# Splits off GpSimd, a second q on ScalarE, and attention steps at other places among the projection's units

## The chip, the cores and the metric

The kernel runs on one core of one Trainium2 chip. The metric is the device time of one execution in microseconds (us), the median of several. Engines are TensorE (PE, with its weight loads as PEld), VectorE (DVE), ScalarE (ACT), GpSimd (POOL) and SyncE (SP), whose queue issues nearly all transfers.

## The reference

A decoder block on 256 tokens of 1024 numbers, float32: an attention mixer, a layer norm, a mixture of 32 experts, a second layer norm. Cut to what matters here:

```python
proj = x @ w_in + b_in                       # q, k, v of mixers A and B, gates
y_a = banded_attention(qa, ka, va, bias_a, 128, sinks)
y_b = g0 * o_cmp + g1 * o_slc + g2 * o_win   # compressed, selected, window branches of mixer B
merged = gate_a * (y_a @ w_branch_a) + gate_b * (y_b @ w_branch_b)
h = layer_norm(alpha * x + merged @ w_out)
logits = h @ w_router + b_router             # top 4 of 32 experts
for each expert e and its tokens:
    u = rows @ w_gate_up[e] + b_gate_up[e]
    out += weight * (swiglu(u) @ w_down[e] + b_down[e])
y = layer_norm(alpha * h + out)
```

Expert weights are 12.6 MB for each of 32 experts, and all are read once.

## The kernel before

The front computes the projection in 32 **units**, n = 0 to 31: a unit is 128 of the 4096 columns, in the order of `order` (four of qa, k, v, two for the compressed branch, k, four of qb, v, k, v, and 16 merge gates). From unit 2 on the product is made of three matmuls for each of 8 row blocks, with x and w each split in a high part (rounded to fp32r) and a low part (the rest), so 24 matmuls of 128x256 in a unit. `split_w` makes these parts for unit n + 2 while unit n runs (`AHEAD`): `round_split` (L193) casts the high part on ScalarE and subtracts on DVE; where `POOL_PART` says "h" GpSimd makes the high part (L196), where it says "l" GpSimd subtracts (L200). Three pairs of weight tiles take turns (`NWS`).

A unit yields after its fourth and after its eighth row block. These **steps** h = 0 to 63 are where the attention's work is put in: `PLAN` names for each step what is called there. `Sbr` is the scores of branch b (0 is mixer A, 1 the selected branch, 2 the window) and head pair r: eight matmuls into two of three PSUM banks (`ps_s`), four DVE operations that add the bias and take the maximum, four exponentials on ScalarE. `N` is the norm (reciprocal on DVE, four multiplications on GpSimd), `T` six transposes on TensorE and two copies, `V` the product with V into the one bank of `ps_y`, which is read as `y` before the next `V`. `vt` are V's transposes, `cp` the compressed branch's products, `ct` a transpose (`pct`), `bl`, `bs`, `bw`, `br` the load, split, store and reload of the experts' biases, `sig` the sigmoids of the first four merge gates, `bias1` the load of a Toeplitz bias.

In this loop only TensorE's and SP's instructions stand in the order in which the code calls them; those of DVE, ScalarE and GpSimd are placed by a scheduler, for the most part as their inputs are expected to be there. Every engine runs its own instructions in order.

At step `END_H` the attention's buffers are given back, and three slots of 2 MB for expert weights (`ringb`) stand in their place. `PRE` says at which steps loads of expert weights are issued ahead; ten slots can be filled before the experts run. After the units come the branch products (`pb`), the output projection (`po`), the router, and the experts in turn, each with four loads of 2 MB (`wg`) and two (`wd`). All of these loads stand in SP's queue in one order, each waiting for its slot.

Of the kernel before, what the change touches and what calls it, by code (L numbers as in the profile page):

```python
# [20 lines left out]
P = 128  # L21
# [12 lines left out]
NRA, NRB, NRP = 3, 3, 1  # L34
WARM = 6
NWS, NSB, AHEAD, SIG0 = 3, 6, 2, 20
POOL_PART = {6: 'h', 7: 'l', 8: 'h', 9: 'l', 10: 'h', 11: 'h', 12: 'h', 14: 'h', 15: 'h', 16: 'l', 17: 'l', 18: 'l', 19: 'h', 20: 'h', 21: 'h', 22: 'h', 23: 'h', 24: 'h', 25: 'h', 27: 'l', 28: 'l', 30: 'l', 38: 'l'}
SIDE_R = "right"
LOADS, LOADS2 = 6, 11
END_H = 36  # L40
SPLIT = 672
SPLIT1 = 512
AHEAD2 = (2, 2, 2, 2, 2, 2, 1, 0)
# [1 line left out]
TWO = 4  # L45
LN_ROWS = {9 + i: (0, i) for i in range(4)} | {20 + i: (1, i) for i in range(4)}
E_RES = 13
PLAN = {7: 'gates', 8: 'sinks', 9: 'c1', 10: 'gsum S00 S02', 11: 'S01 N00 N01', 12: 'N02', 13: 'T00 S03 N03 bias1 T02', 14: 'vt0 V00 T01', 15: 'V01 blocks', 16: 'V02 T03', 17: 'V03 mlp bl', 19: 'gelu', 20: 'bs', 22: 'bw', 23: 'ckv S10 N10', 24: 'S11 N11 br', 26: 'S12 T10 N12', 27: 'T11 S13 N13', 28: 'vt1 csm', 29: 'T12 V11 S20', 30: 'V10 T13 N20', 31: 'ct V13 vt2', 32: 'S21 V12 T20 cp1 cp0 S22 N22 V20 S23', 33: 'N21 T21 N23', 34: 'cp2 cp3 V21 T22', 35: 'rw V22 T23', 36: 'x V23', 38: 'sel', 39: 'sig'}
PRE = {26: 1, 39: 1, 41: 1, 48: 1, 64: 1, 71: 1, 72: 2, 73: 2}


C_BQA, C_BQB, C_BK, C_BV, C_BC, C_PK, C_W2K, C_W2V, C_WN = 0, 4, 8, 11, 14, 16, 48, 112, 176
# [7 lines left out]
def tile_block(ctx: ExitStack, tc: tile.TileContext, a, out):  # L60
    nc = tc.nc
    PE, DVE, ACT, POOL, SP = nc.tensor, nc.vector, nc.scalar, nc.gpsimd, nc.sync
# [124 lines left out]
    mp = er.enter_context(tc.tile_pool(name="mp", bufs=1, side=SIDE_R))  # L187
# [67 lines left out]
    pk = mp.tile([P, NPK], F32, name="pk")  # L255
# [67 lines left out]
    qT = {}  # L323
# [37 lines left out]
    def prep(n):  # L361
        while prepped[0] <= min(n, len(jobs) - 1):
            k = prepped[0]
            prepped[0] += 1
            parts[k] = split_w(jobs[k](), f"j{k}", POOL_PART.get(k, ""), 2 if k < TWO else 1)

    z2 = []
    mg = {}
    def unit(n):

        issue(n + (LOADS if n < 10 else 12))
        if n >= MAN:
            prep(n + AHEAD)

        wh, wl = parts.pop(n) if n >= MAN else (chunk(0)[:, n], None)
        k = order[n]
        t = w_tile(f"pu{n}")
        for j in range(NJ):
            if n < MAN:
                PE.matmul(t[:, :S], wh[:, j, :], xT[:, j, :], start=(j == 0), stop=(j == NJ - 1))  # L380
            else:
                mm3(t[:, :S], wh[:, j, :], wl[:, j, :], xh[:, j, :], xl[:, j, :], j == 0, j == NJ - 1)
            if j == 3:
                yield
        t = t[:, :S]
        if k[0] == "q":
            c = (C_BQA, C_BQB)[k[1]] + k[2]
            if k[2] == 0:
                qT[k[1]] = mp.tile([P, 4, S], F32, tag="qT", name=f"qT{k[1]}")
            DVE.tensor_scalar(qT[k[1]][:, k[2], :], t, pk[:, c:c + 1], 0.125, ALU.add, ALU.mult)  # L390
        elif k[0] == "k":
            b = k[1]
            kT[b] = mp.tile([P, S + 15], F32, tag=f"kT{b % 2}", name=f"kT{b}")
            ACT.activation(kT[b][:, kof[b]:kof[b] + S], t, AF.Identity, bias=pk[:, C_BK + b:C_BK + b + 1])
        elif k[0] == "v":
            b = k[1]
            vt = pp.tile([P, S], F32, tag="vt", bufs=1, name=f"vt{b}")
            ACT.activation(vt, t, AF.Identity, bias=pk[:, C_BV + b:C_BV + b + 1])
            vts[b] = vt
        elif k[0] == "c":  # L400
            if not z2:
                z2.append(mp.tile([P, 2, 2, P], F32, tag="tz", name="z2"))

            s = k[1]
            tv = t.rearrange("p (u two) -> p two u", two=2)
            for par in range(2):
                for g in range(2):
                    DVE.tensor_scalar_add(z2[0][64 * par:64 * par + 64, s, g, :], tv[64 * g:64 * g + 64, par, :],
                                          pk[64 * g:64 * g + 64, C_BC + s:C_BC + s + 1])
# [19 lines left out]


    bd = dram.tile([3, P, 768], BF16, name="bd")
    bt = []

    def bias_load():
        bt.append(mp.tile([P, 2048], F32, name="bt"))
        SP.dma_start(bt[0][:, :512], a["b_gu"].rearrange("e (q c) -> (e q) c", q=4))
        SP.dma_start(bt[0][:, 512:768], a["b_d"].rearrange("e (q c) -> (e q) c", q=4))

    def bias_split():
        f = bt[0][:, :768]  # L440
        b3 = bt[0][:, 768:1920].bitcast(BF16).rearrange("p (k c) -> p k c", k=3)
        for k in range(3):
            (DVE.tensor_copy if k == 2 else ACT.copy)(b3[:, k], f)
            if k < 2:
                DVE.tensor_tensor(f, f, b3[:, k], ALU.subtract)

    def bias_store():
        b3 = bt[0][:, 768:1920].bitcast(BF16).rearrange("p (k c) -> p k c", k=3)
        SP.dma_start(bd.rearrange("k p c -> p k c"), b3)

    def bias_rows():
        SP.dma_start(bparts, bd.rearrange("k (e q) c -> (k e) (q c)", q=4))
# [273 lines left out]
    for b in range(3):  # L726
        steps[f"vt{b}"] = lambda b=b: v_transpose(b)
        steps[f"bias{b}"] = lambda b=b: load_T(b)
        for r in range(4):
            p = pairs[b][r]  # L730
            steps[f"S{b}{r}"], steps[f"N{b}{r}"], steps[f"T{b}{r}"], steps[f"V{b}{r}"] = p.scores, p.norm, p.transpose, p.pv
    for r in range(4):
        steps[f"cp{r}"] = lambda r=r: cmp_pv(r)
    plan = {k: [steps[x] for x in v.split()] for k, v in PLAN.items()}
    h = 0
    for n in range(len(order)):
        for _ in unit(n):
# [12 lines left out]
    for mt in range(8):  # L750
        if mt % 2 == 0:
            n = len(order) + mt
            issue(n + 1 + LOADS2)
            prep(n + 1 + AHEAD)
            wb = [parts.pop(n), parts.pop(n + 1)]
        preload(PRE.get(64 + mt, 0))
        t = w_tile(f"pb{mt}")
        k = (mt % 2) * P
# [7 lines left out]
        if mt % 4 == 3:  # L766
# [16 lines left out]
    sel = cp.tile([P, 2, E], F32, name="sel")  # L783
# [360 lines left out]
    for e in range(E):  # L1144
        x, p = ex[e], (ex[e - 1] if e else None)
# [88 lines left out]
    with tc.For_i(0, nrun, 1) as e:  # L1234
# [13 lines left out]
        for tt in range(2):  # L1248
            t_ = slice(tt * P, (tt + 1) * P)
            for jj in range(2):  # L1250
                t = ps_w.tile([P, 512], F32, tag="w0", name=f"vht{tt}{jj}")
# [5 lines left out]
            for hf in range(2):  # L1257
# [7 lines left out]
                t = ps_w.tile([P, 512], F32, tag="w0", name=f"vt{tt}{hf}")  # L1265
# [116 lines left out]
```

## Time and profile before

| | us |
|---|---|
| median of 3 runs | 1139.63 (1136.96 to 1140.21) |
| the profiled execution | 1138.73 |
| its span | 1137.0 |
| start of unit 18's second half, behind the last attention step | 118.32 |
| end of the units | 157.3 |

Times in the profile count from the start of the span. The busy share of TensorE counts an engine's instructions from start to end, and matmuls overlap, so it is an upper bound of work.

### The profile page before, as it was taken

What the parts mean: (1) busy time and instruction counts of PE and PEld (TensorE: products, weight loads), DVE (VectorE), ACT (ScalarE), POOL (GpSimd) and SP (SyncE); (2) the same over time, 40 slices, a digit from 0 to 9 for tenths busy, and PEclk for the clock granted to TensorE, in tenths of its full rate; (3) what the DMA queues carried; (4) which work ended last, traced back from release to release, by engine and by line L of the source; (5) the groups of instructions that cost most, each with busy time, mean ns of one, the idle gap of its engine ahead of it and who ended that gap; (6) DMA issues with size and microseconds to landing.
All of it is one profiled execution on the core that took longest, in us unless ns stands there. A gap on an engine that the chain in (4) does not pass through costs nothing.

```text
span 1137.0 us, 13456 instructions
## 1 busy us (share of the span) xinstructions
PE 1069.5 (94%) x5660; PEld 511.0 (45%) x5660; DVE 293.1 (26%) x710; ACT 203.8 (18%) x434; POOL 78.9 (7%) x115
## 2 busy tenths in 40 slices
PE   9799999999999999999999998998999998989895
PEld 7686998643434343434343333333333333333321
DVE  3777447312111111111121211111020202010213
ACT  3446244220111011111110101010111110001011
POOL 1435310000000000000000000000000000000001
PEclk9899999999999999899999999999999999999998
DMA  8562777699999999999999999999999999999993
GB/s 317 208 243 115 316 295 305 264 423 427 428 426 428 427 428 427 428 426 429 426 427 427 429 427 427 427 428 427 428 426 428 427 428 426 428 427 428 428 427 126
DMA packets 36848, 438.50 MB, mean 386 GB/s; under 512 B 3872, under 2 KB 6576, under 8 KB 9008
## 3 DMA queue, kind: packets, MB, share of 16 engines
q1 hardware_dynamic: 36448, 436.98, 92.0%
q8 instruction: 46, 0.75, 0.3%
q10 hardware_dynamic: 336, 0.62, 0.2%
q14 instruction: 18, 0.15, 0.0%
HBM read 435.92 MB, written 1.66 MB: 385 GB/s over the span
## 4 chain that ended last, share of the span: by engine, by line


## 5 line engine op out<-in xcount | busy, mean ns | idle before, releaser
L1099 PE MATMUL g<-wg,xeM 128*64 128x512 f32 x2048 | 474.7, 604 | 3.7 <-DMA wg<-in_w_gu_dram 3.6
L1099 PEld LDWEIGHTS g<-wg,xeM 128*64 128x64 f32 x2048 | 141.3, 138 | 265.2 <-issue 236.6
L1121 PE MATMUL pd<-wd,wk 128*64 128x512 f32 x1024 | 228.9, 594 | 28.7 <-DMA wd<-in_w_d_dram 28.7
L1121 PEld LDWEIGHTS pd<-wd,wk 128*64 128x64 f32 x1024 | 73.7, 137 | 174.3 <-issue 140.2
L1126 DVE COPY y<-pd 64x512 f32<-64x512 f32 x32 | 22.2, 693 | 428.6 <-ACT y L1125 428.6
L1079 DVE TENSOR_SCALAR gs<-g 128x512 f32<-128x512 f32 x32 | 22.1, 692 | 246.7 <-PE g L1099 246.7
L1125 ACT COPY y<-pd 64x512 f32<-64x512 f32 x32 | 18.5, 578 | 296.1 <-PE pd L1121 296.1
L224 PE MATMUL pu<-xhl,w_j 128*128 128x256 f32 x240 | 70.7, 294 | 0.0
L225 PE MATMUL pu<-xhl,w_j 128*128 128x256 f32 x240 | 68.4, 285 | 0.0
L226 PE MATMUL pu<-xhl,w_j 128*128 128x256 f32 x240 | 68.3, 285 | 0.0
L1013 POOL TENSOR_SCALAR wk<-const,posm 128x64 f32<-128x64 f32 x30 | 12.8, 445 | 798.0 <-PE pst L1068 793.9
L1054 PEld LDWEIGHTS px<-wk,h_tok 128*128 128x128 f32 x480 | 55.8, 191 | 24.3 <-DVE gs L1079 12.2
L1054 PE MATMUL px<-wk,h_tok 128*128 128x128 f32 x480 | 61.6, 281 | 0.0
L1075 PE MATMUL yac<-y,wk 128*128 128x512 f32 x128 | 59.2, 605 | 0.7 <-ACT y L1125 0.7
L1110 ACT COPY wk<-pa 128x512 f32<-128x512 f32 x32 | 18.8, 586 | 196.8 <-PE pa L1109 185.3
L224 PEld LDWEIGHTS pu<-xhl,w_j 128*128 128x128 f32 x240 | 46.6, 194 | 2.0 <-issue 1.2
L225 PEld LDWEIGHTS pu<-xhl,w_j 128*128 128x128 f32 x240 | 46.5, 194 | 0.0
L226 PEld LDWEIGHTS pu<-xhl,w_j 128*128 128x128 f32 x240 | 46.4, 194 | 0.0
L1081 ACT ACTIVATE wk<-gs 128x512 f32<-128x512 f32 x31 | 19.5, 629 | 149.3 <-DVE gs L1079 149.2
L1075 PEld LDWEIGHTS yac<-y,wk 128*128 128x128 f32 x128 | 23.0, 189 | 36.7 <-issue 34.7
L1000 ACT ACTIVATE xeM<-px,const 128x128 f32<-128x128 f32 x64 | 24.1, 457 | 74.5 <-PE px L1054 73.1
L202 DVE TENSOR_TENSOR w_j<-w,w_j 128x1024 fp32r<-128x1024 f32 (+1 forms) x24 | 29.1, 1222 | 25.9 <-ACT w_j L198 15.3
(230 smaller groups left out, 852.2 us busy)
## 6 DMA issues: line engine op xcount, KB each, us to landing
wg<-in_w_gu_dram SPq DMA_DIRECT2D x128, 2048.0 KB, 38.0
wd<-in_w_d_dram SPq DMA_DIRECT2D x63, 2048.0 KB, 39.1
w<-in_w_in_dram SPq DMA_DIRECT2D x14, 1024.0 KB, 8.6
w_br<-in_w_branch_dram SPq DMA_DIRECT2D x4, 1024.0 KB, 8.6
w_o<-in_w_out_dram SPq DMA_DIRECT2D x4, 1024.0 KB, 6.7
T<-ud SPq DMA_DIRECT2D x2, 1024.0 KB, 7.0
w_c<-in_w_c_dram SPq DMA_DIRECT2D x2, 1024.0 KB, 16.7
wd<-in_w_d_dram SPq DMA_DIRECT2D x2, 1024.0 KB, 35.5
```

What stands on the lines that cost most here:

```text
L202: DVE.tensor_tensor(lo, src, hi.bitcast(F32), ALU.subtract)
L224: PE.matmul(o_, wh, xh, start=start, stop=False)
L225: PE.matmul(o_, wh, xl, start=False, stop=False)
L226: PE.matmul(o_, wl, xh, start=False, stop=stop)
L1000: ACT.activation(o_, src, AF.Identity, bias=b_, scale=g_)
L1054: PE.matmul(t[:, k * P:(k + 1) * P], h_tok[:, tt, j * P:(j + 1) * P], oh[:, tt].rearrange("p k s -> p (k s)"), start=(tt == 0), stop=(tt = ...
L1075: PE.matmul(yac[tt][o_], st[:, tt * P:(tt + 1) * P], y2[:, o_, :], start=first, stop=last)
L1079: DVE.tensor_scalar_min(g_, gate_, LIMIT)
L1081: ACT.activation(s_, g_, AF.Sigmoid, scale=SW_ALPHA)
L1099: PE.matmul(self.g[b][64 * hf:64 * hf + 64, :], xes[e][:, j, :], w[:, 1024 * b + 512 * hf:1024 * b + 512 * hf + 512], start=False, stop=(j ...
L1121: PE.matmul(d[64 * o_:64 * o_ + 64, :], aT[:, P * j + 64 * hf:P * j + 64 * hf + 64], w[:, 1024 * j + 512 * o_:1024 * j + 512 * o_ + 512], ...
L1126: DVE.tensor_copy(y2[k, 1, :], d[CAP:])
```

## The change

`POOL_PART` keeps only units 21 to 25, all "h": units 2 to 20 and those from 26 on are split by ScalarE and DVE alone. The bias of q is scaled once by 0.125, and the four units of the second q are read from PSUM by ScalarE instead of DVE. The experts' biases are loaded into tiles of the merge gates (`M[0, 1]`, `M[1, 1]`) and a late tile instead of one of their own, and split, stored and reloaded at steps 40, 43 and 46 instead of 20, 22 and 24. The other entries of `PLAN` are spread over steps 10 to 39 instead of 10 to 36, `sig` stands at 40 instead of 39, the buffers are given back at step 39, and two preloads come one step later.

```diff
-POOL_PART = {6: 'h', 7: 'l', 8: 'h', 9: 'l', 10: 'h', 11: 'h', 12: 'h', 14: 'h', 15: 'h', 16: 'l', 17: 'l', 18: 'l', 19: 'h', 20: 'h', 21: 'h', 22: 'h', 23: 'h', 24: 'h', 25: 'h', 27: 'l', 28: 'l', 30: 'l', 38: 'l'}
+POOL_PART = {k: 'h' for k in range(21, 26)}
-END_H = 36
+END_H = 39
-PLAN = {7: 'gates', 8: 'sinks', 9: 'c1', 10: 'gsum S00 S02', 11: 'S01 N00 N01', 12: 'N02', 13: 'T00 S03 N03 bias1 T02', 14: 'vt0 V00 T01', 15: 'V01 blocks', 16: 'V02 T03', 17: 'V03 mlp bl', 19: 'gelu', 20: 'bs', 22: 'bw', 23: 'ckv S10 N10', 24: 'S11 N11 br', 26: 'S12 T10 N12', 27: 'T11 S13 N13', 28: 'vt1 csm', 29: 'T12 V11 S20', 30: 'V10 T13 N20', 31: 'ct V13 vt2', 32: 'S21 V12 T20 cp1 cp0 S22 N22 V20 S23', 33: 'N21 T21 N23', 34: 'cp2 cp3 V21 T22', 35: 'rw V22 T23', 36: 'x V23', 38: 'sel', 39: 'sig'}
-PRE = {26: 1, 39: 1, 41: 1, 48: 1, 64: 1, 71: 1, 72: 2, 73: 2}
+PLAN = {7: 'gates', 8: 'sinks', 9: 'c1', 10: 'gsum S00', 11: 'S01', 12: 'N00 vt0', 13: 'S02 N01 T00', 14: 'T01', 15: 'S03 N02 V00 bias1', 16: 'T02 V01', 17: 'N03 V02 bl', 18: 'T03 blocks', 19: 'V03', 20: 'mlp', 21: 'gelu', 23: 'ckv S10', 24: 'S11 N10', 25: 'N11 T10', 26: 'S12', 27: 'T11 N12', 28: 'vt1 S13', 29: 'V10 T12 N13 csm', 30: 'V11 S20', 31: 'T13 V12', 32: 'S21 N20 vt2 ct', 33: 'V13 T20 N21 cp0', 34: 'S22 V20 T21 cp1', 35: 'S23 N22 V21', 36: 'T22 N23 cp2 cp3', 37: 'V22', 38: 'T23', 39: 'V23 rw x', 40: 'sig sel bs', 43: 'bw', 46: 'br'}
+PRE = {26: 1, 40: 1, 42: 1, 48: 1, 64: 1, 71: 1, 72: 2, 73: 2}
...
-            DVE.tensor_scalar(qT[k[1]][:, k[2], :], t, pk[:, c:c + 1], 0.125, ALU.add, ALU.mult)
+            if n == 0:
+                DVE.tensor_scalar_mul(pk[:, C_BQA:C_BQA + 8], pk[:, C_BQA:C_BQA + 8], 0.125)
+            if k[1]:
+                ACT.activation(qT[1][:, k[2], :], t, AF.Identity, bias=pk[:, c:c + 1], scale=0.125)
+            else:
+                DVE.tensor_scalar(qT[0][:, k[2], :], t, 0.125, pk[:, c:c + 1], ALU.mult, ALU.add)
...
     def bias_split():
-        f = bt[0][:, :768]
-        b3 = bt[0][:, 768:1920].bitcast(BF16).rearrange("p (k c) -> p k c", k=3)
+        b3.append(M[1, 1].rearrange("p a b -> p (a b)")[:, :768].bitcast(BF16).rearrange("p (k c) -> p k c", k=2))
+        b3.append(late.tile([P, 384], F32, tag="tm", name="b3").bitcast(BF16))
         for k in range(3):
-            (DVE.tensor_copy if k == 2 else ACT.copy)(b3[:, k], f)
+            b_ = b3[1] if k == 2 else b3[0][:, k]
+            (DVE.tensor_copy if k == 2 else ACT.copy)(b_, bt)
             if k < 2:
-                DVE.tensor_tensor(f, f, b3[:, k], ALU.subtract)
+                DVE.tensor_tensor(bt, bt, b_, ALU.subtract)
```

Three places show how instructions move. The first is TensorE behind unit 5's first half, at step 10; `s_0_0` and `s_0_1` are the two banks of S00, `s_2_...` those of S02, `s_1_...` those of S01, `pu` a unit. Before:

```order
L314 MATMUL pngs<-const,gp 128x24 x2
L593 MATMUL s_0_0_331<-kT_302,qT_176 128x256
L593 MATMUL s_0_1_332<-kT_302,qT_176 128x256
L593 MATMUL s_0_0_331<-kT_302,qT_176 128x128
L593 MATMUL s_0_1_332<-kT_302,qT_176 128x128
L593 MATMUL s_2_0_352<-kT_302,qT_176 128x256
L593 MATMUL s_2_1_353<-kT_302,qT_176 128x256
L593 MATMUL s_2_0_352<-kT_302,qT_176 128x128
L593 MATMUL s_2_1_353<-kT_302,qT_176 128x128
L224 MATMUL pu_310<-xhl,w_j_230 128x256
```

Of the change, S00 and what follows it, and the end of unit 5 with S01:

```order
L314 MATMUL pngs<-const,gp 128x24 x2
L599 MATMUL s_0_0_332<-kT_303,qT_176 128x256
L599 MATMUL s_0_1_333<-kT_303,qT_176 128x256
L599 MATMUL s_0_0_332<-kT_303,qT_176 128x128
L599 MATMUL s_0_1_333<-kT_303,qT_176 128x128
L224 MATMUL pu_311<-xhl,w_j_231 128x256
```

```order
L225 MATMUL pu_311<-xhl,w_j_231 128x256
L226 MATMUL pu_311<-xhl,w_j_231 128x256
L599 MATMUL s_1_0_367<-kT_303,qT_176 128x256
L599 MATMUL s_1_1_368<-kT_303,qT_176 128x256
L599 MATMUL s_1_0_367<-kT_303,qT_176 128x128
L599 MATMUL s_1_1_368<-kT_303,qT_176 128x128
L224 MATMUL pu_393<-xhl,w_j_272 128x256
```

The second pair of scores stood directly behind the first; now 12 matmuls of unit 5 lie between them.

The second place is ScalarE near T03 and V03: `pT_3_1` is T03's second copy, `bt` (now `M_73` and `M_75`) the experts' biases, `yhl` the read of a `V`. Before:

```order
L198 CAST yhl<-y_1_569 128x256
L198 CAST yhl<-y_2_599 128x256
L648 COPY pT_3_1_616<-t_3_1_612 128x384
L443 CAST bt<-bt 128x768
L394 ACTIVATE kT_630<-pu_586,pk 128x256
L198 CAST yhl<-y_3_632 128x256
L443 CAST bt<-bt 128x768
```

Of the change:

```order
L198 CAST yhl<-y_2_608 128x256
L449 CAST M_75<-M_73 128x768
L654 COPY pT_3_1_643<-t_3_1_639 128x384
L393 ACTIVATE qT_663<-pu_620,pk 128x256
L198 CAST w_j_678<-w_388 128x1024
L449 CAST M_75<-M_73 128x768
L198 CAST yhl<-y_3_665 128x256
```

The first cast of the biases stood behind the copy for V03 and now stands ahead of it; it has not gone behind the attention.

The third place is ScalarE at the last pairs of branch 2: `sb` are exponentials, `M_72` and `M_74` the first merge gates. Before:

```order
L614 ACTIVATE sb_3_1_1265,su_3_1261<-sb_3_1_1265,st_3_1260 128x128
L648 COPY pT_1_1_1302<-t_1_1_1298 128x384
L702 ACT_TABLE_LOAD
L702 ACTIVATE M_72<-M_72 128x256
L648 COPY pT_2_1_1352<-t_2_1_1348 128x384
L198 CAST yhl<-yB 128x256
L702 ACTIVATE M_74<-M_74 128x256
```

Of the change:

```order
L708 ACT_TABLE_LOAD
L708 ACTIVATE M_74<-M_74 128x256
L654 COPY pT_2_1_1361<-t_2_1_1357 128x384
L198 CAST yhl<-yB 128x256
L620 ACT_TABLE_LOAD
L620 ACTIVATE sb_3_0_1309,su_3_1308<-sb_3_0_1309,st_3_1307 128x256
L620 ACTIVATE sb_3_0_1309,su_3_1308<-sb_3_0_1309,st_3_1307 128x128
L620 ACTIVATE sb_3_1_1312,su_3_1308<-sb_3_1_1312,st_3_1307 128x256
L620 ACTIVATE sb_3_1_1312,su_3_1308<-sb_3_1_1312,st_3_1307 128x128
L708 ACT_TABLE_LOAD
L708 ACTIVATE M_72<-M_72 128x256
```

The sigmoids stood behind the last exponential, with one table load; now they stand between exponentials, and before S22's exponentials a further pair of loads stands in the same way, so that there are five.

## Rows read from the trace of the kernel before

**Rows 1.** The page: the span, the busy time of each engine with its share, and GB/s in 40 equal slices.

```profile
span 1137.0 us, 13456 instructions
PE 1069.5 (94%) x5660; PEld 511.0 (45%) x5660; DVE 293.1 (26%) x710; ACT 203.8 (18%) x434; POOL 78.9 (7%) x115
GB/s 317 208 243 115 316 295 305 264 423 427 428 426 428 427 428 427 428 426 429 426 427 427 429 427 427 427 428 427 428 426 428 427 428 426 428 427 428 428 427 126
```

**Rows 2.** Stretches: from:to, length, then busy us (and instructions) of PE, PEld, DVE, ACT, POOL; then the granted clock, the DMA engines' busy share, GB/s.

```profile
26.00:118.30 92.30, 81.30 (x685) 67.76 (x683) 70.42 (x242) 44.16 (x143) 44.31 (x62) 0.96 0.55 206
118.30:157.30 39.00, 39.00 (x327) 38.98 (x326) 14.07 (x14) 13.94 (x22) 12.46 (x8) 1.00 0.85 331
157.30:209.00 51.70, 51.40 (x371) 46.98 (x370) 36.80 (x68) 22.49 (x30) 3.27 (x3) 1.00 0.69 265
209.00:220.00 11.00, 11.00 (x69) 6.16 (x69) 4.79 (x26) 3.62 (x8) 0.85 (x2) 1.00 0.51 191
220.00:1137.00 917.00, 862.47 (x4074) 330.46 (x4070) 156.85 (x340) 110.74 (x219) 16.00 (x32) 0.99 0.98 417
```

**Rows 3.** Waits of TensorE from 20 to 120 us: what waited, for whom, us in total, times, longest.

```profile
PE s L593 <- DVE st L604: 3.8, 1, 3.8
PE y L661 <- DVE V L428: 1.9, 1, 1.9
PE pct L549 <- DVE pT L650: 1.2, 1, 1.2
PE t L643 <- POOL sb L636: 1.2, 3, 0.5
```

**Rows 4.** Waits with the same columns: of TensorE from 220 us on, of SP's queue from 100 to 260 us, of ScalarE from 20 to 120 us.

```profile
PE pd L1121 <- DMA wd<-in_w_d_dram: 28.7, 25, 2.1
...
SPq L78 <- DVE w_j L202: 93.2, 8, 30.1
...
ACT sb L614 <- DVE st L611: 13.3, 6, 5.7
```

**Rows 5.** Stretches around the longest wait, columns as in rows 2.

```profile
27.90:31.80 3.90, 0.06 (x2) 0.01 (x2) 3.90 (x8) 0.24 (x1) 2.02 (x1) 0.82 1.02 429
30.35:37.20 6.85, 5.41 (x22) 4.65 (x24) 4.02 (x24) 2.97 (x13) 0.81 (x1) 0.50 0.88 367
37.20:59.00 21.80, 18.03 (x160) 14.78 (x160) 17.92 (x52) 10.90 (x40) 11.66 (x20) 1.00 0.37 119
```

**Rows 6.** The timelines of GpSimd and DVE, where both work: start, us, engine, line, operation.

```profile
27.59 2.34 POOL L200 TENSOR_TENSOR w_j<-w,w_j 128x1024 fp32r<-128x1024 f32 x1
27.66 3.35 DVE L202 TENSOR_TENSOR w_j<-w,w_j 128x1024 fp32r<-128x1024 f32 x1 [3.30 <-POOL w_j L196]
44.79 1.89 DVE L629 TENSOR_TENSOR su<-su,st 128x4 f32<-128x4 f32 x1
89.72 2.36 POOL L200 TENSOR_TENSOR w_j<-w,w_j 128x1024 fp32r<-128x1024 f32 x1
89.81 2.54 DVE L542 TENSOR_TENSOR pc<-c_s,c_m 128x240 f32<-128x240 f32 x1
```

**Rows 7.** Groups of instructions to 240 us: line, engine, operation, shapes, count, busy us, mean ns of one, idle time before them.

```profile
L198 ACT CAST w_j<-w 128x1024 fp32r<-128x1024 f32 x14 | 14.4, 1038 | 2.5 <-DMA w<-in_w_in_dram 2.4
L614 ACT ACTIVATE sb<-sb,st 128x256 f32<-128x256 f32 x24 | 12.0, 500 | 17.1 <-DVE st L611 13.3 <-DVE st L609 3.8
L604 DVE CUSTOM_DVE_ANT_0 sb<-s,T 128x256 f32<-128x256 f32 x24 | 10.0, 417 | 6.2 <-PE s L593 6.2
L202 DVE TENSOR_TENSOR w_j<-w_o,w_j 128x1024 fp32r<-128x1024 f32 x8 | 9.8, 1221 | 5.0 <-ACT w_j L198 5.0
L390 DVE TENSOR_SCALAR qT<-pu,pk 128x256 f32<-128x256 f32 x8 | 3.9, 483 | 4.1 <-PE pu L226 2.5 <-DMA pk<-in_pk_dram 1.4
```

**Rows 8.** Timelines: the cast of unit 7's or 6's high part when its chunk is there; the scores of S03 behind T00; those of S10; T10; four norms of a pair; the second half of unit 18, behind V23.

```profile
26.45 1.04 ACT L198 CAST w_j<-w 128x1024 fp32r<-128x1024 f32 x1 [1.06 <-DMA w<-in_w_in_dram]
42.41 0.49 PE L593 MATMUL s<-kT,qT 64*128 64x256 f32 x2
70.33 0.50 PE L593 MATMUL s<-kT,qT 64*128 64x271 f32 x2
78.24 0.33 PE L643 MATMUL t<-const,sb 128*128 128x128 f32 x1 [0.45 <-POOL sb L636]
83.82 1.63 POOL L636 TENSOR_SCALAR sb<-sb,su 128x256 f32<-128x256 f32 x4 [2.88 <-ACT pT L648]
118.32 0.39 PE L224 MATMUL pu<-xhl,w_j 128*128 128x256 f32 x1
```

**Rows 9.** ScalarE's timeline at the sigmoids.

```profile
110.66 1.28 ACT L702 ACT_TABLE_LOAD   x1
111.95 0.42 ACT L702 ACTIVATE M<-M 128x256 f32<-128x256 f32 x1
```

**Rows 10.** Timelines of SP's queue and of ScalarE: the Toeplitz load that waits for S03's read, the second load of the biases, their first cast.

```profile
47.26 0.38 SPq L278 DMA_DIRECT2D T<-ud  x1
...
48.78 0.46 SPq L437 DMA_DIRECT2D bt<-in_b_d_dram  x1
...
57.05 0.83 ACT L443 CAST bt<-bt 128x768 bf16<-128x768 f32 x1
```

More of the change, by code (lines that the diff above doesn't have):

```diff
@@ L431, in tile_block @@
     bd = dram.tile([3, P, 768], BF16, name="bd")
-    bt = []
+    bt, b3 = M[0, 1].rearrange("p a b -> p (a b)")[:, :768], []
     def bias_load():
-        bt.append(mp.tile([P, 2048], F32, name="bt"))
-        SP.dma_start(bt[0][:, :512], a["b_gu"].rearrange("e (q c) -> (e q) c", q=4))
-        SP.dma_start(bt[0][:, 512:768], a["b_d"].rearrange("e (q c) -> (e q) c", q=4))
+        SP.dma_start(bt[:, :512], a["b_gu"].rearrange("e (q c) -> (e q) c", q=4))
+        SP.dma_start(bt[:, 512:768], a["b_d"].rearrange("e (q c) -> (e q) c", q=4))
     def bias_split():
-        f = bt[0][:, :768]
-        b3 = bt[0][:, 768:1920].bitcast(BF16).rearrange("p (k c) -> p k c", k=3)
+        b3.append(M[1, 1].rearrange("p a b -> p (a b)")[:, :768].bitcast(BF16).rearrange("p (k c) -> p k c", k=2))
+        b3.append(late.tile([P, 384], F32, tag="tm", name="b3").bitcast(BF16))
         for k in range(3):
-            (DVE.tensor_copy if k == 2 else ACT.copy)(b3[:, k], f)
+            b_ = b3[1] if k == 2 else b3[0][:, k]
+            (DVE.tensor_copy if k == 2 else ACT.copy)(b_, bt)
             if k < 2:
-                DVE.tensor_tensor(f, f, b3[:, k], ALU.subtract)
+                DVE.tensor_tensor(bt, bt, b_, ALU.subtract)
     def bias_store():
-        b3 = bt[0][:, 768:1920].bitcast(BF16).rearrange("p (k c) -> p k c", k=3)
-        SP.dma_start(bd.rearrange("k p c -> p k c"), b3)
+        SP.dma_start(bd.rearrange("k p c -> p k c")[:, :2], b3[0])
+        SP.dma_start(bd[2], b3[1])
     def bias_rows():
```

## The prediction

> **What bounds the kernel now.** I read the page's slices first. From the eighth slice on the core's DMA engines move 417 to 428 GB/s and stay there to the end, while TensorE counts as busy 94% of the span [rows 1]. Then the stretches: from 220 us on DMA is 0.98 busy; before it, in no stretch over 0.85 [rows 2]. The waits from 220 us on say the same from TensorE's side: its longest is for expert weights (`wd`), 28.7 us, and the SP queue, in which the loads stand, waits before that time for slots to come free, 93.2 us for the splits alone [rows 4]. So the kernel has two parts: a front to about 220 us, in which transfers wait for buffers and so for TensorE's progress, and an expert stretch of 917 us whose end is its start plus a fixed number of bytes at a fixed rate. A microsecond saved in the front moves every later slot and so the end by one; a microsecond that some engine saves beside TensorE moves nothing.
>
> Within the front, from 118.3 us to 157.3 us TensorE is busy 39.00 of 39.00 us: 13.5 units of 2.89 us (327 matmuls, 0.119 us apart). In the next stretch 0.3 us are missing. All slack lies between 26 and 118.3 us: busy 81.30 of 92.30, and a mean clock of 0.96 [rows 2]. The waits name it: 3.8 us for DVE's reading of scores, 1.9 us for V, 1.2 for `pct`, 1.2 for norms on GpSimd [rows 3]. The 3.8 us end at 31.8; in them the granted clock falls to 0.50, 1.2 GHz, and stays there from 30.35 to 37.2 us: 6.85 us, so 3.4 us of matmul time lost [rows 5]. What can be won is thus 11.0 + 3.4 = 14.4 us; the change has to be followed through this stretch alone.
>
> **The change, part by part.** *GpSimd out of the splits.* Of units 6 to 20 nine high parts (1.04 us each) go from GpSimd to ScalarE, five low parts go to DVE (1.22 us each) [rows 7]. DVE gets time back too: its low part beside GpSimd's of the next unit took 3.35 us, an addition of 128x4 numbers 1.89 and the `pc` product 2.54 beside others [rows 6]. Where GpSimd splits nothing they would take some 1.2, 0.2 and 0.5, so these three alone lost 5.9 us; shorter ones beside GpSimd's casts lost perhaps 3 more, an estimate. So DVE gains 9 us and, for four q units of 0.48 us, 1.9, and takes 6.1; ScalarE takes 9.4 + 1.9 us.
>
> *Bias split.* The plan moves it to steps 40 to 46, but only SP and TensorE follow the plan's order here; the order rows show the first cast still ahead of the third pair's `pT` copy, as nearly before. It even stands one place earlier, so `pT` now queues behind the landing of the bias rows. This part does not do what it says, except for the store and reload (2 x 0.59 MB), which meet a queue with room (0.85 busy, [rows 2]): nothing.
>
> *Sigmoids.* They moved to step 40 and the scheduler pulled three between the last exponentials: five table loads where there was one, 4 x 1.28 = 5.1 us of ScalarE [rows 9], on the path of the last two pairs. The Trainium skill (ScalarE: Activation LUTs, "Table sets: the hidden batching unit") speaks against this: batch functions by set; "What ACT_TABLE_LOAD costs" gives 2.66 us a switch with a drain. The trace disagrees on size: the sigmoid starts 1.29 us after the load [rows 9]. By the page's figure ScalarE would take 10.6 us, an estimate, and the sum below would end some 3 us later.
>
> *q through ScalarE* and the scaling of `pk` (one small DVE operation) stand beside units that TensorE already runs; nothing, and at most their own 0.5 us if ScalarE is the late one. *END_H and PRE:* three preloads come 4.3 us later in units, in a stretch with 0.15 of DMA free; nothing, at most the 4.9 us of one 2 MB load at 428 GB/s if the queue were full.
>
> **The sum.** I followed the changed order by hand from 26.6 us, every instruction with the duration of its row: a pair's scores on DVE 1.2 us, its four exponentials 1.9, its four norms 1.63, a cast 1.04, a low part 1.22 [rows 7, 8], half a unit 1.43 (1.5 with the switch). Three milestones have the same content before and after.
>
> 1. *Start of the work behind T00* (units 0 to 6, S00, S01, S02, T00): 42.41 us before [rows 8]. After: ScalarE casts units 6 and 7 from 26.45 us [rows 8], DVE takes their low parts without the 3.35 us, reads S00 from 30.0; the bank that S01 needs is free at 30.7. TensorE comes at 29.0, waits 1.6 instead of 3.8, and I take the clock to stay (it was 1.00 through the 1.9 us wait, [rows 5]; a fall would cost 3.4). T00 then waits 1.5 us, since z's four additions lie ahead of the denominators on DVE, and 0.8 more for the norms' pace. It ends at 38.2: **4.2 us won.**
>
> 2. *Start of S10* (units 0 to 11, all of branch 0): 70.33 before [rows 8]. After, every pair is asked for about 5 us after its scores, and its chain takes longer: T01 2.1 us late, V01 1.5 (its one PSUM bank waits for DVE's low part of y0, queued behind the scores of S03), V02 0.8, T03 1.7. V03 1.5: SP issues the Toeplitz load when S03 is read, 49.1 us instead of 47.2, so the bias rows, which were cast at 57.05, 8.3 us after their issue at 48.78 [rows 10], are there at 58.9 (that the one was 8.3 us behind the other is carried over), and the copy that V03 needs ends at 60.2. That is 7.6 us against some 4 before. S10 starts at 69.5: **0.8 us still won.**
>
> 3. *End of V23.* Before, 118.32 with 18.5 units done [rows 8]; after, the plan has 20 by then, 36 more matmuls or 4.3 us. From S10's scores to T10 the chain took 7.9 us [rows 8] with seven half units and scores to fill it; now two halves and S11 fill 4.8 of some 6.6: 2.2 us late. Then S11 0.3, V11 0.7, V20 1.3 and T23 1.7 (both behind table loads), T22 and V22 0.7: 6.9 us, against about 6.9 that the rows of before hold there with short waits counted. V23 ends at 121.6, which is 117.3 in content of before: **1.0 us won.**
>
> Behind it 12 units run without a gap as 13.5 did. The profiled execution took 1138.73 us, 1.73 us more than its span; less 1.0 that is 1137.7. It lies 0.9 us under the median of the runs shown, 1139.63, so the time that I forecast is 1138.6. A measurement of this kernel tells about 0.3%, 3.4 us, from no change: this is no change.
>
> **The rivals.** *DVE's relief carries (faster).* The waits at T01, V01, T03 and T10 are all DVE or ScalarE being late by 1 to 2 us. If their queues run 1.5 us ahead of my account at each, five such waits vanish, 7 us, and the time is 1131.6. For it: 9 us of port trouble gone from an engine busy 70 of 92 us [rows 2]. Against: DVE's work falls only by some 5 us, while ScalarE's rises by 16.
>
> *The clock falls again (no change or slower).* Nine waits of 0.8 to 1.6 us stand where there was one of 3.8. If one lowers the clock as at 30.35 us, 3.4 us go: 1142.0. Against it: the clock was 1.00 through the 1.9 us wait and after it [rows 5].
>
> *ScalarE bounds the end of the attention (slower).* From the exponentials of S21 to V23 it has 19.6 us of work, five table loads in it, where TensorE has 20. I let it wait little between. Before, it waited 13.3 us in all for DVE ahead of its exponentials [rows 4]; if a third of that falls here, V23 comes 5 us later: 1143.6. It decides from the point where ScalarE reaches S23's exponentials after 117 us. By the page's 2.66 us a load this would hold with no further waits.
>
> **How the numbers follow.** Forecast 0.50, own range 1135.5 to 1141.5; relief 0.30; clock 0.07; ScalarE 0.13. Faster by over 0.3% (under 1136.2) is the relief case and a little of the forecast's edge, 0.32; slower (over 1143.0) the ScalarE case and some of the clock's, 0.17; the rest, 0.51, within. The range reaches from the relief case to the ScalarE case, 1131.0 to 1144.0: the halves of both that lie outside make 2 in 10. The ends of the small edits (0.5, 3.4 and 4.9 us) lie in it.
>
> **What would show it.** Right: no low clock before 220 us; S01's second bank waits about 1.6 us; T00 and T01 wait for norms; ScalarE idle before the bias cast until about 59 us; S10 near 69.5; five table loads between 95 and 120 us; V23's end near 121.6; the units without a gap behind it; DMA full from about 219 us. Wrong: a low clock, waits of TensorE for `w_j`, or V23's end more than 3 us from 121.6. If V23 lies as said and the end does not follow it, then the first paragraph is wrong.

## The result: 15 us slower

The changed kernel takes 1153.43 us (median of 6, 1150.78 to 1155.64), the kernel before, timed beside it, 1138.30 us (median of 6): ratio 1.0136, 95% interval 1.0112 to 1.0160. The forecast was no change, 1138.6 us, 1131.0 to 1144.0. The profiled execution of the change took 1154.85 us. Of all executions behind the times below one was of another kind, one of x2's twelve, which took 4822 us and is left out of x2's ratio.

The page after, to be read against [rows 1]: the span and the busy times, then GB/s in 40 slices.

```profile
span 1153.1 us, 13468 instructions
PE 1072.6 (93%) x5660; PEld 513.2 (45%) x5660; DVE 292.2 (25%) x716; ACT 219.7 (19%) x451; POOL 50.1 (4%) x97
GB/s 338 164 244 138 169 335 285 239 371 422 429 426 427 426 427 426 427 429 425 427 427 428 429 428 427 427 426 427 427 427 427 428 428 427 427 427 429 427 425 121
```

The full rate begins one slice later than before; from there on hardly anything differs. So the loss is in the front. TensorE's waits there, from 26 to 128 us and then from 128 to 176 us (columns as in [rows 3]):

```profile
PE t L649 <- POOL sb L642: 5.7, 5, 1.9
PE y L667 <- DVE yhl L202: 2.2, 2, 1.4
PE t L651 <- POOL sb L642: 2.0, 2, 1.1
PE s L599 <- DVE st L610: 1.4, 1, 1.4
...
PE pu L224 <- ACT M L421: 6.8, 1, 6.8
```

The last of these rows has no counterpart before: [rows 2] has TensorE busy 39.00 of 39.00 us from the end of the attention to the end of the units. Line 421 is the sigmoid that writes a merge gate. ScalarE's waits from 128 to 160 us and its timeline there say what it waited for, and the SP queue's timeline when that was issued:

```profile
ACT M L421 <- DMA bd<-M: 4.8, 1, 4.8
```

```profile
148.41 0.47 ACT L421 ACTIVATE M<-pu,const 128x256 f32<-128x256 f32 x1 [1.83 <-PE pu L226]
148.79 1.03 ACT L198 CAST w_j<-w 128x1024 fp32r<-128x1024 f32 x1
154.63 0.47 ACT L421 ACTIVATE M<-pu,const 128x256 f32<-128x256 f32 x1 [4.81 <-DMA bd<-M]
```

```profile
115.41 0.38 SPq L690 DMA_DIRECT2D h_tok<-in_x_dram  x1
133.56 0.33 SPq L78 DMA_DIRECT2D w_br<-in_w_branch_dram  x1
134.00 0.37 SPq L78 DMA_DIRECT2D wg<-in_w_gu_dram  x1
134.41 0.44 SPq L78 DMA_DIRECT2D w_br<-in_w_branch_dram  x1
134.90 0.64 SPq L78 DMA_DIRECT2D wg<-in_w_gu_dram  x1
135.58 0.45 SPq L454 DMA_DIRECT2D bd<-M  x1
136.07 0.50 SPq L455 DMA_DIRECT2D bd<-b  x1
155.15 0.32 SPq L458 DMA_DIRECT2D bparts<-bd  x1
```

The store of the split biases (`bd`) reads a tile that unit 25's gate is to overwrite. It is issued at 135.58 us, at most 2.0 us behind two loads of 1 MB and two of 2 MB in the same queue, and the gate can be written at 154.63, 19 us later. ScalarE runs unit 26's gate first, the one at 148.41; unit 27 needs the PSUM bank of unit 25, and for it TensorE stands still from 148.1 us on. Before, the first of those 2 MB loads went out ahead of the branch weights, not behind them:

```profile
111.68 0.43 SPq L684 DMA_DIRECT2D h_tok<-in_x_dram  x1
119.84 0.33 SPq L78 DMA_DIRECT2D wg<-in_w_gu_dram  x1
128.19 0.33 SPq L78 DMA_DIRECT2D w_br<-in_w_branch_dram  x1
```

Stretches of the change with the columns of [rows 2]: three with a low clock in the attention; the units ahead of the wait, the wait, and behind it; last, from the experts' first product to the end.

```profile
31.49:34.90 3.41, 3.41 (x18) 3.41 (x18) 2.14 (x8) 1.92 (x11) 0.00 (x0) 0.50 0.96 401
38.31:41.73 3.42, 3.15 (x14) 2.66 (x15) 3.31 (x15) 1.02 (x3) 1.38 (x3) 0.50 0.02 5
79.27:82.69 3.42, 2.83 (x13) 2.74 (x13) 1.01 (x4) 1.03 (x5) 2.17 (x5) 0.50 0.61 187
...
127.99:148.10 20.11, 20.11 (x170) 20.11 (x169) 9.34 (x11) 5.71 (x10) 3.31 (x4) 1.00 0.68 275
148.10:155.15 7.05, 0.28 (x3) 0.07 (x1) 1.23 (x1) 1.88 (x3) 0.00 (x0) 0.70 0.58 195
155.15:161.19 6.04, 6.04 (x28) 6.04 (x29) 0.00 (x0) 0.51 (x2) 0.00 (x0) 0.50 0.84 263
161.19:172.28 11.09, 11.09 (x94) 11.09 (x94) 4.90 (x4) 5.13 (x7) 0.00 (x0) 1.00 1.01 420
228.69:1153.10 924.41, 866.88 (x4105) 331.96 (x4104) 159.92 (x356) 111.54 (x222) 16.05 (x32) 0.99 0.98 415
```

The wait costs twice: 6.8 us of standing still, and in the 6.04 us behind it the granted clock is 0.50, 1.2 GHz, so that 28 matmuls pass where 51 would pass at full clock (94 in 11.09 us): 2.7 us more. From 127.99 to 172.28 us the 12 units take 44.29 us; without a wait they take 34.63 (x1, below). That is 9.7 of the 15.1 us. The other 5 lie ahead of 128 us.

### The profile page after: what moved, and what is told of

The parts are those of the page before. It is cut to its first block, busy times and chain, and to the rows that moved or that the text cites. A ratio compares the mean times of both kernels' runs of the same rounds, so it can differ in the third digit from the quotient of the medians.

```text
span 1153.1 us, 13468 instructions
## 1 busy us (share of the span) xinstructions
PE 1072.6 (93%) x5660; PEld 513.2 (45%) x5660; DVE 292.2 (25%) x716; ACT 219.7 (19%) x451; POOL 50.1 (4%) x97
## 4 chain that ended last, share of the span: by engine, by line
## 5 line engine op out<-in xcount | busy, mean ns | idle before, releaser
L224 PE MATMUL pu<-xhl,w_j 128*128 128x256 f32 x240 | 74.0, 308 | 6.8 <-ACT M L421 6.8
L225 PE MATMUL pu<-xhl,w_j 128*128 128x256 f32 x240 | 70.5, 294 | 0.0
L226 PE MATMUL pu<-xhl,w_j 128*128 128x256 f32 x240 | 70.3, 293 | 0.0
L1060 PEld LDWEIGHTS px<-wk,h_tok 128*128 128x128 f32 x480 | 55.8, 191 | 24.3 <-issue 12.2
L224 PEld LDWEIGHTS pu<-xhl,w_j 128*128 128x128 f32 x240 | 48.9, 204 | 10.9 <-ACT M L421 7.0
L225 PEld LDWEIGHTS pu<-xhl,w_j 128*128 128x128 f32 x240 | 48.8, 203 | 0.0
L226 PEld LDWEIGHTS pu<-xhl,w_j 128*128 128x128 f32 x240 | 48.6, 203 | 0.0
L202 DVE TENSOR_TENSOR w_j<-w,w_j 128x1024 fp32r<-128x1024 f32 (+1 forms) x32 | 37.0, 1164 | 34.5 <-ACT w_j L198 28.8
```

The lines of the kernel that those rows point to most:

```text
L202: DVE.tensor_tensor(lo, src, hi.bitcast(F32), ALU.subtract)
L224: PE.matmul(o_, wh, xh, start=start, stop=False)
L225: PE.matmul(o_, wh, xl, start=False, stop=False)
L226: PE.matmul(o_, wl, xh, start=False, stop=stop)
L1060: PE.matmul(t[:, k * P:(k + 1) * P], h_tok[:, tt, j * P:(j + 1) * P], oh[:, tt].rearrange("p k s -> p (k s)"), start=(tt == 0), stop=(tt = ...
```

## The experiments

The theory was that the store costs 9.8 us (A), with the attention stretch as the rest; the rival was that the attention or the later loads are the loss and the wait only fills time (B). Behind each time stands its ratio to the kernel before, timed on the same chip.

**x1, the bias steps back.** Up to the experts, SP's order differs from the change's, and on ScalarE unit 25's gate goes ahead of unit 26's again; the orders of the others are the same.

```diff
-20: 'mlp'
+20: 'mlp bs'
+22: 'bw'
-24: 'S11 N10'
+24: 'S11 N10 br'
-40: 'sig sel bs', 43: 'bw', 46: 'br'
+40: 'sig sel'
```

> The changed kernel with the split, store and reload of the biases planned at steps 20, 22 and 24 again; only SP's order differs from the changed kernel's. Theory A (the store: in the changed kernel TensorE waits 6.8 us at unit 27 because unit 25's gate must not overwrite a tile that the bias store still reads, the store being 19 us under way behind 6 MB of loads, and the clock then stays low from 150.95 to 161.19 us, some 3 us more): both go, 9.8 us in all, so about 1143.6 us where the changed kernel takes 1153.4, that is +5 us on the kernel before. Theory B (the attention stretch or the later loads are the loss, the wait only takes up time that something else would): less than 3 us are won, 1150 or more.

Measured: 1142.22 us, 4.75 above before (1.0042, 1.0027 to 1.0057). TensorE has no wait between 128 and 176 us, and the units behind the attention run without a gap, from 124.69 to 159.32 us; the last 31.33 us of that, with the columns of [rows 2]:

```profile
127.99:159.32 31.33, 31.33 (x264) 31.33 (x263) 13.47 (x11) 12.53 (x19) 3.06 (x3) 1.00 0.90 371
```

A holds, to the size: 5 us above before was expected.

**x3, the store alone moved up in SP's queue.** `bw` at step 40 instead of 43, everything else as in the change.

> The changed kernel with only the store's place in SP's queue changed: step 40 instead of 43, so ahead of two loads of 2 MB and one of 1 MB and behind one of 1 MB. Theory A: it is issued near 134 us as in the changed kernel, lands some 5 us later, ahead of unit 25's gate at 146; no wait at unit 27, about 1143.6 us as in the kernel with the bias part back, within 2 us. Rival (what costs is the store so late at all, or the reload that blocks SP's queue until it has landed): the wait shrinks only in part, 1147 to 1153 us.

Measured: 1144.08 us (1.0053, 1.0034 to 1.0072), and no wait behind the attention. SP's timeline shows the store behind one load of 1 MB instead of 6 MB, and the reload, which waits for both parts, 7.5 us after its issue:

```profile
132.88 0.33 SPq L78 DMA_DIRECT2D w_br<-in_w_branch_dram  x1
133.25 0.44 SPq L454 DMA_DIRECT2D bd<-M  x1
133.72 0.47 SPq L455 DMA_DIRECT2D bd<-b  x1
134.31 0.72 SPq L78 DMA_DIRECT2D wg<-in_w_gu_dram  x1
...
140.74 0.33 SPq L458 DMA_DIRECT2D bparts<-bd  x1
```

So it is not that the store comes late in the program, but what stands ahead of it.

**x9, the store as late as in the change, from another tile.** The two parts that lay in unit 25's columns lie in a tile of their own, the third where units 29 and 31 write later.

```diff
-        b3.append(M[1, 1].rearrange("p a b -> p (a b)")[:, :768].bitcast(BF16).rearrange("p (k c) -> p k c", k=2))
-        b3.append(late.tile([P, 384], F32, tag="tm", name="b3").bitcast(BF16))
+        b3.append(late.tile([P, 768], F32, tag="tm", name="b3").bitcast(BF16).rearrange("p (k c) -> p k c", k=2))
+        b3.append(M[1, 1].rearrange("p a b -> p (a b)")[:, 640:1024].bitcast(BF16))
```

> The changed kernel with the store and the reload where the change puts them (steps 43 and 46), but the two parts that lay in unit 25's tile now lie in a tile that nothing writes before the output products, and the third part in the columns of units 29 and 31. The store still lands some 19 us after its issue and the reload still holds SP's queue until then; only unit 25's gate no longer waits for it. If the overwritten tile is what cost: no wait at unit 27, time as with the bias part back, 1142 to 1144. If the queue behind the reload is what cost (branch weights issued near 155 us instead of 142): 1148 or more, with TensorE waiting for branch weights after 160 us.

Measured: 1143.80 us (1.0068, 1.0042 to 1.0094), no wait ahead of unit 27. The store lands 19.5 us after its issue, and the reload, which waits for it, holds SP's queue as long as in the change, 134.81 to 154.41, and the branch weights behind it are as late:

```profile
134.81 0.50 SPq L455 DMA_DIRECT2D bd<-M  x1
154.41 0.32 SPq L458 DMA_DIRECT2D bparts<-bd  x1
154.83 0.36 SPq L78 DMA_DIRECT2D w_br<-in_w_branch_dram  x1
```

TensorE waits 0.3 us in the branch products, for DVE, and for no weights. What cost was the tile that unit 25 overwrites; a cost of the round trip or of the blocked queue is not seen (the intervals of x9 and x1 overlap).

**x2, the bias part alone, put on the kernel before** (its tiles and its steps 40, 43 and 46; the rest as before).

> The kernel before with the bias part alone: biases in tiles of the gates, split, store and reload at steps 40, 43 and 46. Theory A: the store stands behind one 2 MB and two 1 MB loads that are issued from 128.2 us on, so it lands near 139 us, 1 us ahead of unit 25's end at 140; TensorE does not wait, the time is that of before within 1.5 us, and the 9.8 us of the changed kernel come from this part only together with the later END_H and attention steps. Theory A2 (the part costs by itself whatever stands around it): +7 to +10 us on before, with a wait at unit 27.

Measured: 1139.57 us (1.0018, 1.0003 to 1.0034). TensorE's waits behind the attention:

```profile
PE pu L224 <- ACT M L416: 1.9, 1, 1.9
```

The same wait, about a quarter as long, where I had expected none: the store is issued at 122.81 with two loads of 1 MB and one of 2 MB just ahead of it, and the reload follows at 136.85, 14 us later. Behind the wait the granted clock is 0.50 for 3.4 us (from 138.88 us), and from `pgb`, the product for the router's weights, to the branch products x2 takes 46.69 us, before 43.07. So the part costs 3.6 us in the old queue by the trace, 0.3 to 3.9 by the times; with `END_H`, the preloads and the branch weights where the new table puts them, it costs 9.7.

This trace shows something else too. Up to the end of the attention every engine but SP does the same in x2 as before, in the same order; and yet from S00 to `pgb` x2 takes 81.46 us where before takes 87.62. 5.7 us of the difference are there by the end of T00, and it begins with the first wait. GpSimd's high part, which DVE's low part waits for, starts in before when its weights have landed, in x2 2.1 us earlier, and S01's second bank waits 0.3 us instead of 3.8. Before's row, then x2's two:

```profile
26.57 1.05 POOL L196 TENSOR_SCALAR w_j<-w 128x1024 fp32r<-128x1024 f32 x1 [18.94 <-DMA w<-in_w_in_dram]
...
24.48 1.05 POOL L196 TENSOR_SCALAR w_j<-w 128x1024 fp32r<-128x1024 f32 x1 [17.21 <-PE pu L226]
27.71 0.92 PE L593 MATMUL s<-kT,qT 64*128 64x256 f32 x6 [0.30 <-DVE st L604]
```

It was the fastest of x2's twelve executions (1135.77 us). So one order of work gave two attention stretches 6 us apart, and the rows of before, from which the forecast starts, are one draw.

**x4, the new table of GpSimd's splits alone on the kernel before; x7, the change with the old table of steps, `END_H` and preloads.**

> The kernel before with the new table of GpSimd's splits alone; attention steps, biases and q as before. If DVE's relief from sharing with GpSimd (9 us less for DVE by the forecast's account) carries by itself: 4 to 7 us faster than before. If the forecast's sum is right, where the gain at the start came with the scores moved apart: within 2 us of before. If ScalarE's 9.4 us of added casts bound the attention: 2 to 6 us slower.

> The changed kernel with the old table of steps, the old END_H and preloads: splits off GpSimd, the second q on ScalarE and the biases in gate tiles stay. If the steps carry the whole loss: within 2 us of before, as the new table of splits alone was (+0.7). If q on ScalarE or the added splits cost by themselves: 2 to 5 us slower than before.

Measured: x4 1138.19 us (1.0007, 0.9994 to 1.0021), x7 1139.05 us (1.0017, 0.9998 to 1.0036). Neither can be told from before. Idle times of TensorE of more than 0.25 us, from S00 to `pgb`, come to 7.7 us in the trace of x4 where before has 10.6; and 10.2 us of that execution have a low clock, before 6.8, which takes up to 1.7 of the 2.9 us back. That this is DVE's relief is not shown: x2, with GpSimd's old splits, comes to 5.1 us.

**x5, x1 with GpSimd's old table of splits.**

> The kernel with the bias part back (x1, +4.75 us on before, 1142.2) and GpSimd's old table of splits. If what is left of the loss came from ScalarE's and DVE's added splits (waits for norms ahead of T00, T01, T10, T22, T23, 7.8 us in x1): 3 to 5 us faster than x1, near before. If it came from the spread attention steps themselves (TensorE changes 28 times between unit and attention where it changed 20 times, and asks for each pair too early whoever splits): within 2 us of x1, or slower by the 3 us that DVE loses beside GpSimd.

Measured: 1147.95 us (1.0087, 1.0055 to 1.0119), 3 to 5 us slower than x1 (by the two timings of that kernel, here and below). In the profiled execution the clock is low for 17.1 us of the attention, in x1's for 3.4. The waits from 20 to 176 us grow where GpSimd's norms and splits share an engine, and DVE's subtraction beside GpSimd's takes 3.39 us again:

```profile
PE t L649 <- POOL sb L642: 8.2, 3, 3.9
PE pu L224 <- ACT vt L403: 2.2, 1, 2.2
```

```profile
26.04 3.39 DVE L202 TENSOR_TENSOR w_j<-w,w_j 128x1024 fp32r<-128x1024 f32 x1 [4.24 <-POOL w_j L196]
```

So taking the splits off GpSimd is worth a few microseconds under the new steps, how much of it by the clock is open, and none that can be measured under the old ones: the spread steps do not lose because of it.

**x6, x1 with the sigmoids held behind the last exponential** (and called at step 39 instead of 40).

```diff
+        late0 = pp.tile([P, 1], F32, tag="sg", bufs=1, name="sg")
+        DVE.tensor_scalar_mul(late0, pw[3].su[:, 1, 0:1], 0.0)
-            ACT.activation(mg[k], mg[k], AF.Sigmoid)
+            ACT.activation(mg[k], mg[k], AF.Sigmoid, bias=late0)
```

> x1 with the four sigmoids held behind the last exponentials: their bias is a zero that DVE works out from the last pair's sums, so there is one table load at the end of the attention instead of five. If the table loads are on the path of the last two pairs (x1 waits 1.1 us inside T22 and 1.6 us ahead of T23, each behind two loads of 1.28 us): 2 to 3 us faster than x1, 1139.5. If ScalarE has slack there: less than 0.5 us.

Measured: 1140.30 us (1.0028, 1.0009 to 1.0048). Waits of TensorE from 100 to 125 us, x1 and then x6:

```profile
PE t L649 <- POOL sb L642: 1.6, 1, 1.6
PE t L651 <- POOL sb L642: 1.1, 1, 1.1
```

```profile
PE t L649 <- POOL sb L642: 0.8, 1, 0.8
```

TensorE does the same things at the same distance in both up to the scores of S22 (103.77 and 103.30 us); from there to `pgb` x1 needs 20.68 us and x6 18.06, so the trace gives the four added table loads 2.6 us. Since the two intervals overlap, and x1 and x6 were timed on two chips, the pair was timed again on one.

> The kernel with the bias part back (x1) once more, on the same chip as the next one, since their two times (+4.75 and +2.1 us on before) were taken on different days' runs of before. If the table loads cost what the two traces show from S22 on (2.6 us): 2 to 3 us slower than the next. If the difference was chance of the clock: within 1 us of it.

> The kernel with the sigmoids late (x6) once more, as the other half of the pair. Table loads: 2 to 3 us faster than its pair, some 2 us slower than before. Chance: within 1 us of its pair.

Measured: 1143.31 us (1.0060, 1.0041 to 1.0080) and 1139.86 us (1.0030, 1.0016 to 1.0044), 3.4 us apart; their traces give 20.71 and 18.07 us for the same stretch, 2.6 apart again. The table loads are on the path.

**x8, the kernel before with its first scores moved apart.**

```diff
-10: 'gsum S00 S02', 11: 'S01 N00 N01', 12: 'N02', 13: 'T00 S03 N03 bias1 T02'
+10: 'gsum S00', 11: 'S02 N00', 12: 'S01 N02', 13: 'N01 T00 S03 N03 bias1 T02'
```

> The kernel before with one thing from the new table of steps: the second pair of scores no longer directly behind the first (S00 at step 10, S02 at 11, S01 at 12). The forecast's first milestone says that the 3.8 us wait and the low clock behind it fall to 1.5 us without a low clock: 3 to 5 us faster than before. Rival (the wait moves to the transposes and the clock falls elsewhere): within 2 us of before.

Measured: 1139.31 us (1.0013, 0.9994 to 1.0032), no gain. TensorE's waits from 20 to 176 us show the rival: the wait for scores falls from 3.8 us [rows 3] to 1.7, and others come up behind it (idle times of more than 0.25 us come to 11.0 us, before to 10.6; the clock is low for 6.8 us in both).

```profile
PE t L643 <- POOL sb L636: 2.6, 2, 2.1
PE pu L224 <- ACT vt L398: 2.2, 1, 2.2
PE s L593 <- DVE st L604: 1.7, 1, 1.7
```

**x10, x6 with ten steps of the attention asked for later** (T00, T01, V01, V02, T03, V03, T10, T22 and V22 one half unit, V03 behind the work of `mlp` besides, T23 behind V22).

> The kernel with the bias part back and the sigmoids late (x6, 1140.3, waits of 10.7 us from S00 to the end of the attention), with T00, T01, V01, V02, T03, V03, T10, T22 and T23 each asked for one half unit later or behind other work of the same step; END_H and preloads as they were. If TensorE waits because the new table asks for each pair before its norms and copies are done: waits fall to some 5 us and the time by as much, 1135. If DVE, ScalarE and GpSimd are the bound there, the waits come back at the next steps: within 2 us of x6.

Measured: 1141.61 us (1.0049, 1.0030 to 1.0067), not faster than x6. Idle times of more than 0.25 us come to 10.9 us as in x6 (10.7); `phid`, the product behind V03, waits now where V03 did (waits from 20 to 215 us):

```profile
PE t L649 <- POOL sb L642: 6.1, 6, 2.0
PE phid L490 <- DVE pT L656: 2.0, 1, 2.0
```

The clock is low for 10.2 us in this execution and never in x6's front, so the idle times say more than the time. My theory that the new table merely asks for each pair too early falls: asked later, the chain of DVE, ScalarE and GpSimd is late at the next step. None of the twelve runs beat the kernel before.

## Why the prediction was wrong, step by step

**What bounds the kernel: right.** From the experts' first product to the end the change takes 924.41 us, and the kernel before, from 213.32 to 1137.0 us, 923.7. The first product starts 15.37 us later and the span is 16.1 longer. What the front loses, the end loses. (Before, the full rate stands from the ninth slice on, not from the eighth as I read it.)

**The bias part: the step that failed.** It said that the store and reload "meet a queue with room (0.85 busy, [rows 2]): nothing". Two things were left out, and both can be read ahead of time. The first is what the store reads: the diff moves the split parts into `M[1, 1]`, and unit 25 writes there, so a transfer that nobody waited for became one that a gate, and through two PSUM banks TensorE, must wait for. A busy share says how full the queue is on the mean; it does not say who waits for the transfer. The second is what stands ahead of it in SP's queue. I had costed the later preloads (two, not three) at nothing and the store at nothing, each alone; but at step 40 instead of 39 the 2 MB loads fall behind branch weights that wait for a slot until 133.56 us, then all go at once, and the store behind them. 6.3 MB at the 428 GB/s of [rows 1] are 14.7 us by an estimate; 19.0 were measured, the last of the four loads landing at 153.6 us and the store 1.0 us behind it. The Trainium skill (DMA: Bandwidth & Descriptors, "Queues, rings and completion order") has each DMA engine take the descriptors of one queue in their order; the traces agree: 19 us behind 6 MB, 7 us behind 1 MB in x3. No rival had this wait in it, so the range could not hold the result. The change's loss less that of x9, x3, x11 and x1, each against before on its own chip, puts it at 8.5 to 10.4 us, the trace at 9.7.

**The three milestones.** Times from the first scores of S00 (26.60 us before, 25.17 in the change, 25.10 in x6); what follows the three starts at 39.94, 71.50 and 127.75 us in the change and at 37.29, 69.08 and 121.36 in x6; before's third is [rows 8]'s 118.32 with the 36 matmuls (4.3 us) that the change has done by then.

| | before | forecast | x6, no low clock, one table load | the change |
|---|---|---|---|---|
| end of T00 | 15.8 | 11.6 | 12.2 | 14.8 |
| start of S10 | 43.7 | 42.9 | 44.0 | 46.3 |
| end of V23 | 96.0 | 95.0 | 96.3 | 102.6 |

In content the columns differ by 0.3 us at two places: V's first transposes come ahead of the end of T00 only after, `pgb` ahead of the end of V23 only before.

*First milestone.* The waits were right: TensorE waits 1.4 us for S01's second bank (1.6 forecast) and 1.9 ahead of T00, and where the clock stays the work behind T00 begins 3.6 us earlier than in before's trace (4.2 forecast). But that the steps won this is not shown: x2, with the old steps, has the three milestones at 10.1, 38.9 and 89.9 us (the third counted as before's). The forecast took before's 3.8 us wait and its low clock for what that order costs each time. "I take the clock to stay" did not hold in the change: it was low at 31.49 and again at 38.31 us, up to 1.7 us lost each time.

*Second and third.* The gain is given back, as the forecast said, and by 1.1 to 1.3 us more than it said: x6 is 0.3 us behind before at both, where 0.8 and 1.0 us of gain were forecast. Up to S10 TensorE is idle 7.6 us before and 7.9 in x6. What is left when idle times and half of the busy time at the low clock are taken off is 33.4 us before and 33.5 in x2, but 36.0 in x6, 35.4 in x1 and, where the clock was low for over 10 us there, 34.2 in x10 and 33.9 in x5, for the same 320 instructions. By this estimate, which is rough, the new steps lose 0.5 to 2.6 us there in TensorE's own work, while the waits are as long as before. One term of the sum was too small for it: half a unit between other products takes 1.59 us on the mean in x6, where I had 1.5, about 1 us over the 13 halves up to S10. The rest is open. From S10 to V23 I counted 6.9 us of delays on either side; idle times are 3.4 us before and 3.7 in x6. That the difference came out nearly right is luck: both terms were about twice too large. x6, the change without its two large mistakes, is 2 to 3 us slower than before by the times of x6 and x12; x7 without the new steps 0.8, within its interval of nothing.

*Table loads.* Five stood where the forecast saw them, between 106 and 123 us. I had counted 3.0 us for waits behind them, at V20 and T23; in x1 TensorE waits inside T22 (1.1 us) and ahead of T23 (1.6). The traces give 2.6 us in all, the times 2.7 (x1 and x6, on two chips) and 3.4 (the pair on one). The rival "ScalarE bounds the end of the attention" had this place and mechanism, and 5 us. The operation behind a load starts 1.30 us after the load's start in this trace too:

```profile
118.55 1.28 ACT L620 ACT_TABLE_LOAD   x1
119.85 0.51 ACT L620 ACTIVATE sb<-sb,st 128x256 f32<-128x256 f32 x1
```

The Trainium skill (ScalarE: Activation LUTs, "What ACT_TABLE_LOAD costs") counts 2.66 us a switch; no row here shows more than 1.28 us and a pause of some 0.02. Its advice to batch functions by set was right, and its size not seen.

*Rivals.* "DVE's relief carries", 0.30, did not come: x4 has that part alone and is not faster than before. "The clock falls again" had a chance of 0.07 and a loss of 3.4 us. The change had three in the attention, up to 1.7 us each, and a fourth behind the wait for the store, 2.7 us.

**Smaller steps.** q through ScalarE and the scaling of `pk`: nothing that can be told in x7, as said. ScalarE waited for the bias rows until 60.06 us (59 forecast), idle 4.9 us before it:

```profile
60.06 0.83 ACT L449 CAST M<-M 128x768 bf16<-128x768 f32 x1 [4.93 <-DMA M<-in_b_d_dram]
```

Not counted was unit 38's low part, which the new table takes from GpSimd: the branch products, 23.2 us before (157.29 to 180.50), take 23.6 in x1, x4, x6, x7 and x9, with a wait of 0.3 us for DVE.

The account of the 15.1 us: 8.5 to 10.4 for the store's tile, 2.6 to 3.4 for table loads, 2 to 3 for the new steps with all the rest. Of the last, 0.5 to 2.6 us lie, by the estimate above, in TensorE's own work ahead of S10; what makes that work longer is open, for no run changes it alone.

## What to carry to other kernels

When a buffer is moved into a tile that something else writes later, the transfer that reads it gets a deadline: find who writes the tile next, and list what stands ahead of the transfer in its own queue, with the time at which that is free to go, before calling it hidden. Edits that are each free alone (later loads, a later store, a shared tile) must be costed together on the queue that they share. And a wait that is taken away from TensorE counts only if the chain behind it (here maximum, exponential, norm, copy) is done earlier too: x8 and x10 moved waits, and saved nothing. And a wait read off one profiled execution is a draw: look at a second one before a gain is built on its going away.

## What the runs showed of the hardware

The granted clock is not a property of the program alone. x1 and x11 are one program, x6 and x12 another, and up to S22 TensorE does the same things in the same order in all four; x1 has one low stretch (37.9 to 41.3 us), x11 two (from 35.8 and 76.8 us, 3.4 us each), x6 and x12 none in the front. In the change, x3 and x9 TensorE's order is the same too, and they show three such stretches, one and none in the attention. The change and x9 wait 1.4 us each for S01's second bank; the clock is low from 31.49 us in the change, and stays full in x9. So the same wait of 1 to 2 us stands in an execution with a low clock behind it and in one without, and an estimate should carry it as a chance of some 1.7 us for each such wait, not as yes or no. The Trainium skill (TensorE: Matmul & The Clock Gate, "What's actually happening") says of the start of a kernel that the number of slow matmuls differs from run to run; here the start differs too. The first units' matmuls stand 0.43 us apart until 9.9 us in the profiled execution before, and 0.22 us apart from 5.6 us on, where they do not wait, in that of the change, which is why S00 begins 1.4 us earlier in it. The change did nothing for that: in x4, with the old steps, S00 begins at 25.10 us, in x9, with the new ones, at 26.62.
